# Newton's steps of the norm in PSUM, and adaLN slabs ahead of a SwiGLU's earliest quad

## The chip, the cores and the metric

The kernel runs on one core of a Trainium2 chip. The metric is device time in microseconds (us), the median of the runs shown. A core has five engines that work beside each other, each with its own queue of instructions executed in order: PE (products), DVE, ACT and POOL (elementwise work) and SP, which here only issues DMAs. They wait for each other through semaphores. Products write to PSUM, which DVE and ACT can read and write; all else lies in SBUF.

## What is computed

One step of a diffusion backbone of two layers on 640 tokens (512 latent, 128 context) of width 1024. Each layer is a SwiGLU, a mixer and a second SwiGLU, each behind a modulated norm:

```python
def rms_norm(x, g):
    y = x * lax.rsqrt(jnp.mean(x * x, axis=-1, keepdims=True) + EPS)
    return y * g
def modulate(h, shift, scale):
    return h * (1 + scale) + shift
def swiglu(h, w_gate, w_up, w_down):            # width 1024 -> 2816 -> 1024
    return (jax.nn.silu(h @ w_gate) * (h @ w_up)) @ w_down
mod = silu(cond) @ w_ada[l] + b_ada[l]          # nine vectors of 1024 a layer: shift, scale, gate x 3
x = x + 0.5 * mod[2] * swiglu(modulate(rms_norm(x, g[0]), mod[0], mod[1]), ...)
x = x + mod[5] * mixer(modulate(rms_norm(x, g[1]), mod[3], mod[4]))
x = x + 0.5 * mod[8] * swiglu(modulate(rms_norm(x, g[2]), mod[6], mod[7]), ...)
```

The mixers (neighbourhood attention with a recurrence; a Fourier transform) lie outside the change.

## The kernel before

**Tiling.** Channels lie on partitions, eight chunks of 128; the tokens are two halves of 320 columns (h = 0 and 1). A float32 product is three passes: weights and activations are split into a high and a low part, and high x high, low x high and high x low are summed. ACT makes a weight's high part (whi, line 176), DVE the low part (wlo, line 181), from a staging buffer (st) that a DMA on SP's queue fills (line 139). Buffers, and with them the loads, come free when the work that reads them is done; SP issues loads strictly in the planned order.

**Norm.** Sums of squares come from small products into a PSUM bank (nst, line 402). DVE turns three columns of them into 1/sqrt: v (line 415), a first guess on the bits (line 417), then three Newton steps of three operations each (lines 420, 421, 422), all on 128 x 3 values. Three operations spread the factors on a diagonal (dg, line 430), and products with ones bring them to all partitions (nbc, line 453). From nbc each chunk of h is made: x times nbc (line 473, or 469 in one step), the modulation (lines 476 and 479), the high part hh (lines 471 and 481) and the low part hl (lines 492 and 495).

**SwiGLU.** The inner width is 22 chunks. Chunks 0 and 1 are done directly in `ffn_body`: four units of weights (gate and up of each) times half 0 and then times half 1, in steps n as the norm gives chunks of h. Chunks 2 to 21 are "quads": gate and up of one chunk form a 2 x 2 matrix for Strassen's and Winograd's seven products. A quad's weights need sums (POOL, lines 226, 227, 231, 232) and six steps that split them (A1's whi and wlo come first). `prep(upto, 1)` takes one such step. The token side needs sums too (line 528, POOL and DVE) and their splits (th line 171, tl line 172). `norm_steps` is a generator that yields after each chunk; it is called for half 1 while the products of half 0 run: at step n = 1 DVE's Newton for half 1 is queued, at n = 4 nbc and the first three chunks, and the rest one chunk at each step of half 1, where PE takes each as it comes. Half 0's own SiLU (line 728) and product (729) come between the third and the fourth chunk of half 1.

**Slabs.** The nine vectors a layer are products with w_ada, cut in 144 slabs of 512 KB, eight to a vector (`fill`, line 327). They have no place of their own but fill PE's gaps. Three of the four SwiGLUs place some: 0ffn2 (layer 0, second; half 1's norm near 846 us of the trace), 1ffn1 (near 1315) and 1ffn2 (near 1861). `FILLS` gives for these the slabs at the first four steps of half 1 (two each; one each in 1ffn2) and after each quad. `plan_ffn` writes the order of the loads: in before the earliest quad's gate and up, then these eight (four) slabs, then the rest.

Of the kernel before, what the change touches and what calls it, by code (L numbers as in the profile page):

```python
# [32 lines left out]
class Item:  # L33
    """weights of one product: their loads, the steps that split them, what the steps made"""
# [7 lines left out]
class Kern:  # L42
# [21 lines left out]
    def buffers(self, pool, phase, n_st, n_w):  # L64
        """buffers for weights: as loaded, and split; those of a phase serve its weights only"""
        for j in range(n_st):
            self.st_free.append((pool.tile([P, 1024], F32, name=f"st{j}"), phase))
        for j in range(n_w):
            self.w_free.append((pool.tile([P, 1024], F32R, name=f"whi{j}"),
                                pool.tile([P, 1024], F32R, name=f"wlo{j}"), phase))  # L70
# [14 lines left out]
    def slab_pool(self, st, upto, bufs=2):  # L85
        """weights of the adaLN vectors: slabs up to this one are used in the phase"""
        self.slab_p = st.enter_context(self.tc.tile_pool(name="slab", bufs=bufs))
        self.s_dma = self.s_use
        self.s_end, self.s_bufs = upto, bufs

    def psum(self, pairs):
        """PSUM of a phase: six single banks or three pairs"""
        if self.ps_pairs is pairs:
            return
        self.ps_st.close()
        self.ps_pairs = pairs
        ps = self.ps_st.enter_context(self.tc.tile_pool(name="ps", bufs=3 if pairs else 6, space=PSUM))
        if pairs:
            self.pair = lambda name: ps.tile([P, 2, 512], F32, tag="mm", name=name)
            self.bank = lambda name: self.pair(name)[:, 0, :]  # L100
        else:
            self.bank = lambda name: ps.tile([P, 512], F32, tag="mm", name=name)
# [48 lines left out]
    def prep(self, upto, most=99):  # L151
        """steps for the items up to this one, as far as there are buffers"""
        self.flush()
        self.load()
        while self.steps and most:
            it, fn, need = self.steps[0]
            if it.idx >= min(upto, self.limit) or len(it.raw) < len(it.src) and fn in (self.split_w, self.quad_a, self.fold_a):
                return
            w = None
            if need:  # L160
                w = self.pick(self.w_free if need == 1 else self.s1_free, it.slots)
                if w is None:
                    return
            self.steps.pop(0)
            self.flush()
            fn(it, w)
            most -= 1
            self.load()
# [5 lines left out]
    def split_later(self, it, hi, lo, src, then=None):  # L174
        """the low part comes with the next step"""
# [20 lines left out]
    def fold_a(self, it, w):  # L196
        """rows m and -m: sum and difference"""
# [12 lines left out]
    # a pair of units as a 2 x 2 matrix (unit, half of the rows): the seven left factors of Strassen and Winograd  # L210
# [59 lines left out]
    def done(self, most=99):  # L270
        """the oldest unit in use is no longer needed"""
# [3 lines left out]
    def mm3(self, out, w, ks, xs, first=True, last=True):  # L275
        """out (+)= W^T X in three passes; w: (hi, lo) as [P, k, 128], xs: k -> (hi, lo)"""
# [8 lines left out]
    def mm_side(self, outs, ws, h, lag=0):  # L285
        """products of several units with half h, chunk after chunk as the norm gives them; the last two unit by unit
        lag: chunks by which the last unit stays behind"""
# [57 lines left out]
    def ada_end(self):  # L345
        """the finished vector, channels on partitions"""
# [28 lines left out]
    def parts(self, h):  # L375
        """pieces of a token half with one condition: (column slice, condition)"""
# [20 lines left out]
    def norm_s(self, h, bank=None):  # L397
        """sums of squares, tokens on partitions"""
# [6 lines left out]
    def norm_a(self, h):  # L405
        """rsqrt(mean(x^2) + eps)"""
# [4 lines left out]
    def rsqrt(self, ps, n=3):  # L411
        """rsqrt(mean(x^2) + eps) of n columns of sums"""
        nc = self.nc
        v, s, t_ = (self.t2.tile([P, 3], F32, tag=t, name=t)[:, :n] for t in ("nv", "ns", "nt"))
        nc.vector.tensor_scalar(out=v, in0=ps[:, 0:n], scalar1=1.0 / D, scalar2=EPS, op0=ALU.mult, op1=ALU.add)
        # the exponent halved on the bits, then Newton's steps
        nc.vector.tensor_scalar(out=s.bitcast(I32), in0=v.bitcast(I32), scalar1=-0.5, scalar2=float(0x5F3759DF),
                                op0=ALU.mult, op1=ALU.add)
        for _ in range(3):
            nc.vector.tensor_tensor(out=t_, in0=s, in1=s, op=ALU.mult)  # L420
            nc.vector.scalar_tensor_tensor(out=t_, in0=t_, scalar=-0.5, in1=v, op0=ALU.mult, op1=ALU.mult)
# [16 lines left out]
    def T_pool(self, ks=range(4)):  # L438
        """right factors of Strassen and Winograd beside the parts of h"""
# [9 lines left out]
    def norm_r(self):  # L449
        """the factors of the tokens on all partitions"""  # L450
# [6 lines left out]
    def norm_high(self, h, l, i, c, r, keep):  # L457
        """h = rms_norm(x) g (1 + scale) + shift and its high part
        keep: for the products of a SwiGLU"""
# [24 lines left out]
    def direct(self, l, i, h, c, keep):  # L484
        """the high part comes without the sum of product and shift"""
# [19 lines left out]
    def norm_steps(self, h, l, i, keep=False):  # L505
        """a step for each chunk, low parts one step behind"""
# [17 lines left out]
    def t_sums(self, k, b12, b22):  # L524
        """T1 = B12 - B11, T2 = B22 - T1, T3 = B22 - B12, T4 = B21 - T2"""
# [21 lines left out]
    # slabs of a SwiGLU: after chunks of the first units, and after each quad  # L547
# [5 lines left out]
    def plan_ffn(self, l, n, s):  # L553
        """weights of a SwiGLU in the order of their use; s: the first slab, returns the next"""
# [22 lines left out]
        for bi, nb in enumerate(BLK):  # L577
            end = min(sum(BLK[:bi + 1]) + 1, NF)
            while f < end:
                self.add_quad(gt[f], up[f], ph, f == 2)  # L580
                if f == 2:
                    slabs(sum(first))
                slabs(rest[f - 2])
# [7 lines left out]
    def ffn(self, l, i, after, mid=iter(()), late=None):  # L591
        """after(h, c): what follows the last update of chunk c, half h; mid: steps of other work, one in each quad;
        late: what follows the last quad"""
# [14 lines left out]
    def ffn_start(self, evac):  # L608
        """the first products of all: the first two vectors of adaLN come chunk by chunk, the norm and the products follow"""
# [7 lines left out]
        def ada(c):  # L617
            """the vectors' values for a chunk, four sums in groups of columns"""
# [102 lines left out]
    def ffn_body(self, l, i, fills, qfills, after, mid, late):  # L721
# [14 lines left out]
        if fills:  # L736
            us = [self.unit() for _ in range(4)]
            for h in range(2):
                ps = [self.bank("pg") for _ in us]
                for n, j in self.mm_side([p[:, :HT] for p in ps], us, h, 0 if h else LAG):  # L740
                    if j == 3:
                        self.prep(self.n_use + 1, 1)
                    if j == 3 and h == 0:
                        if n == 1:
# [5 lines left out]
                    elif j == 3:  # L750
                        step(1)
                        if n < 4:
# [44 lines left out]
    def down_last(self, fs, gate, after):  # L797
        """the last product before a norm: half 0 is through while four chunks of half 1 remain
        the first sums wait for the last chunk of the inner width"""
# [20 lines left out]
    def quad(self, f, fills, begin=False):  # L820
        """gate and up of a chunk, both halves of the tokens, in seven products
        M1 = A11 B11, M2 = A12 B21, M3 = S4 B22, M4 = A22 T4, M5 = S1 T1, M6 = S2 T2, M7 = S3 T3;
        C11 = M1 + M2, U2 = M1 + M6, C12 = U2 + M5 + M3, C21 = U2 + M7 + M4, C22 = U2 + M7 + M5"""
# [73 lines left out]
    def out_last(self, xs, gate, after):  # L897
        """the last product before a norm: half 0 is through while four chunks of half 1 remain"""
# [32 lines left out]
    def mix_setup(self):  # L931
        """parameters of the mixer, log_sigmoid(lambda)"""
# [13 lines left out]
        # y = |lam|, w = exp(-y) by halving steps and a series  # L946
# [17 lines left out]
        # log1p(w) = 2 artanh(w / (2 + w))  # L964
# [11 lines left out]
        # -2 log_sigmoid = 2 (2 artanh) - 2 min(lam, 0)  # L976
# [24 lines left out]
    def lru(self, c, xc, gel):  # L1001
# [21 lines left out]
        for d in range(2):  # L1023
            # exp(-z) and t = tanh(z / 2): 1 - a = t (1 + a), 1 - a^2 = t (1 + a)^2
# [28 lines left out]
    def qk_norm(self, which, c, ps):  # L1053
        """RMS norm over each head's 64 channels; q also gets -1/8"""
# [47 lines left out]
    def mixer0(self, after):  # L1102
        nc, tc = self.nc, self.tc
        self.bg, self.fg = [], []
        with ExitStack() as st:
# [18 lines left out]
            with ExitStack() as s2:  # L1124
# [60 lines left out]
                def early():  # L1185
                    """work that the first tiles of the attention cover"""
# [41 lines left out]
    def bias(self, c, v):  # L1228
        """mask less position bias of a variant of the windows' columns"""
# [122 lines left out]
    def fourier_const(self):  # L1352
        """the DFT matrices in the place of the right factors, a step for each piece"""
# [18 lines left out]
        def steps():  # L1372
# [9 lines left out]
            # the shift times the root of the number of tokens, by chunk in the group, group, condition  # L1382
# [10 lines left out]
    def scaled(self, h, c):  # L1393
        """x g (1 + scale) in parts; the factors of the tokens follow the channels' transform"""
# [12 lines left out]
    def fourier_front(self, const):  # L1407
        """what follows the updates before the transform"""
# [25 lines left out]
    def tok_rest(self):  # L1434
        """factors of the other tokens; the third tile has the end of half 0 and the start of half 1"""
# [8 lines left out]
    def fourier(self, after):  # L1444
        nc, tc = self.nc, self.tc
        NP, NQ, MP, MQ = self.NP, self.NQ, self.MP, self.MQ
        with ExitStack() as st:
# [6 lines left out]
            with ExitStack() as s2:  # L1454
# [11 lines left out]
                def chan(k, g):  # L1466
                    """the channels' transform: token tile k, group g"""
# [9 lines left out]
                def chan_out(k, g):  # L1477
                    """times the factors of the tokens, in parts"""
# [26 lines left out]
                # the shift's part, the same for all tokens  # L1505
# [25 lines left out]
                def pos(r):  # L1531
                    """rows r: cosines of group r, 4 the Nyquist channels, 5 + g sines of group g"""
# [9 lines left out]
                    def shift(q):  # L1542
                        """the shift stays at the first position"""
# [18 lines left out]
            with ExitStack() as s2:  # L1562
# [14 lines left out]
                for c in range(KD):  # L1577
# [17 lines left out]
                    # token n has the sum, the one as far from the end the difference  # L1595
# [16 lines left out]
    def run(self, stop=99):  # L1612
        nc, a = self.nc, self.a
        const = self.const
        with self.tc.manual_schedule():
# [54 lines left out]
            def after(l, i, first=4, per=3, keep=True):  # L1670
                """the next norm: half 0 while the last products of half 1 run"""
# [49 lines left out]
def pack(inp):  # L1721
    """lays the inputs out; no arithmetic"""
# [9 lines left out]
    # the first two vectors by chunks of channels  # L1732
# [47 lines left out]
    # DFT matrices: channels (columns: cosines 0..127, the first halved, cosine 128, sines 1..127) and positions  # L1780
# [37 lines left out]
```

## Time and profile before

| what | us |
|---|---|
| median of 3 runs (2305.37 to 2310.3) | 2305.5 |
| span of the profiled execution | 2305.0 |
| PE, PE weight load, DVE busy | 2224.0, 2110.0, 1554.8 |
| ACT, POOL busy | 990.7, 954.9 |
| PE waiting for dg ahead of nbc, 7 times, the longest | 7.8, 3.4 |
| PE waiting for wlo with pg's products, 3 times, the longest | 5.0, 2.6 |

Busy rows count how long an engine had an instruction in work. A row of the timeline is start, duration, engine, line, operation, output<-input, and in brackets how long the engine had been idle and what ended it. A row of the waits is who waited <- for whom: us in total, times, the longest. A group's row gives count and minimum/median/maximum duration in ns. A row of DMA issues ends with the median us from issue to landing; a row of a stage's window gives the busy times of PE, PE's weight loads, DVE, ACT and POOL, the clock granted to PE (1.00 is full), the share of the DMA engines and GB/s.

### The profile page before, as it was taken

How to read it: one execution, taken by the hardware profiler on the slowest of the kernel's cores; microseconds unless marked ns; L12 is line 12 of the kernel's file. 1: busy time of each engine (PE TensorE's matmuls, PEld its weight loads, DVE VectorE, ACT ScalarE, POOL GpSimd, SP SyncE). 2: the span in 40 equal slices, each digit the busy share in tenths (PEclk: the TensorE clock that was granted, in tenths of full speed). 3: DMA queues.
4: the chain of work that ended last, by engine and by line, in shares of the span. 5: the costliest groups of instructions: out<-in, count | busy, mean ns of one | idle time of the engine just before them, and what ended most of it. 6: DMA issues, size and time to landing. Idle time of an engine off the chain costs nothing.

```text
span 2305.0 us, 39901 instructions
## 1 busy us (share of the span) xinstructions
PE 2224.0 (96%) x15534; PEld 2110.0 (92%) x15534; DVE 1554.8 (67%) x2871; ACT 990.7 (43%) x1780; POOL 954.9 (41%) x856
## 2 busy tenths in 40 slices
PE   7999999999998899999999999999999989999999
PEld 5889999999994788999999889999999979999999
DVE  6676677666865368666666786666667786666665
ACT  4433333347855435333333453333335553333332
POOL 2444444440023235444444454444443645444441
PEclk9999999999999999999999999999999999999999
DMA  7333333321228424333322243332332322222221
GB/s 278 113 111 105 105 107 107 115 74 56 73 71 267 131 83 137 110 101 110 106 91 97 75 155 120 110 97 96 103 117 62 128 85 83 83 83 83 83 89 57
DMA packets 75316, 245.44 MB, mean 106 GB/s; under 512 B 8756, under 2 KB 12996, under 8 KB 75128
## 3 DMA queue, kind: packets, MB, share of 16 engines
q1 hardware_dynamic: 74168, 241.28, 31.7%
q8 instruction: 123, 2.02, 0.4%
q10 hardware_dynamic: 864, 1.38, 0.2%
q14 instruction: 65, 0.53, 0.1%
q0 software_dynamic: 96, 0.22, 0.0%
HBM read 239.71 MB, written 3.15 MB: 105 GB/s over the span
## 4 chain that ended last, share of the span: by engine, by line
PE 79%; DVE 13%; ACT 4%; issue 2%; POOL 2%; DMA 1%; ACTq 0%; DVEq 0%; SPq 0%; POOLq 0%
PE q L282 40%; PE pd L282 26%; PE pj L282 5%; DVE wlo L181 2%; PE ada L327 2%; DVE tl L172 1%; PE pg L282 1%; PE gt L1014 1%; PE pos L1549 1%; DVE x L381 1%; PE S L1262 1%; DVE y L473 1%; DVE sx L1268 1%; PE PT L1288 1%; DMA st<-w_ada 1%
## 5 line engine op out<-in xcount | busy, mean ns | idle before, releaser
L181 DVE TENSOR_TENSOR wlo<-st,whi 128x1024 fp32r<-128x1024 f32 (+2 forms) x401 | 498.4, 1254 | 11.1 <-ACT whi L176 10.2
L176 ACT ACTIVATE whi<-st 128x1024 fp32r<-128x1024 f32 (+2 forms) x405 | 401.2, 992 | 233.0 <-POOL st L232 139.3
L282 PE MATMUL pd<-g,whi 128*128 128x320 f32 x1536 | 347.0, 310 | 4.3 <-DVE u L825 2.3
L381 DVE SCALAR_TENSOR_TENSOR x<-pd,mods,x 128x128 f32<-128x128 f32 (+2 forms) x696 | 265.0, 433 | 111.7 <-PE pd L282 111.2
L282 PE MATMUL q<-hh,wlo 128*128 128x320 f32 x960 | 296.9, 309 | 5.3 <-DVE wlo L181 5.3
L282 PE MATMUL q<-hh,whi 128*128 128x320 f32 x960 | 300.7, 313 | 1.0 <-DVE u L825 1.0
L282 PE MATMUL q<-th,whi 128*128 128x320 f32 x960 | 297.3, 310 | 3.0 <-DVE sg L825 3.0
L282 PE MATMUL q<-tl,whi 128*128 128x320 f32 x960 | 296.6, 309 | 0.7 <-POOL tl L172 0.7
L282 PE MATMUL q<-th,wlo 128*128 128x320 f32 x960 | 296.6, 309 | 0.0
L282 PE MATMUL q<-hl,whi 128*128 128x320 f32 x960 | 296.3, 309 | 0.0
L231 POOL TENSOR_TENSOR st<-sums,st 128x512 f32<-128x512 f32 x80 | 118.0, 1474 | 396.9 <-DVE wlo L181 359.5
L825 POOL TENSOR_TENSOR u<-u,u 128x320 f32<-128x320 f32 x80 | 106.5, 1331 | 401.0 <-DVE u L825 401.0
L282 PEld LDWEIGHTS pd<-g,whi 128*128 128x128 f32 x1536 | 256.8, 188 | 8.9 <-DVE x L381 3.1
L282 PE MATMUL pd<-hh,whi 128*128 128x320 f32 x768 | 238.4, 310 | 0.0
L282 PE MATMUL pd<-hl,whi 128*128 128x320 f32 x768 | 237.9, 310 | 0.0
L282 PE MATMUL pd<-g,wlo 128*128 128x320 f32 x768 | 237.7, 310 | 0.0
L282 PE MATMUL pd<-hh,wlo 128*128 128x320 f32 x768 | 236.8, 308 | 0.0
L826 ACT ACTIVATE sg<-sg 128x320 f32<-128x320 f32 x160 | 75.4, 471 | 284.5 <-DVE sg L825 284.5
L282 PEld LDWEIGHTS q<-hh,whi 128*128 128x128 f32 x960 | 180.2, 188 | 16.8 <-issue 8.6
L282 PEld LDWEIGHTS q<-th,whi 128*128 128x128 f32 x960 | 180.3, 188 | 6.6 <-issue 4.7
L282 PEld LDWEIGHTS q<-hh,wlo 128*128 128x128 f32 x960 | 180.2, 188 | 6.4 <-DVE wlo L181 6.4
L282 PEld LDWEIGHTS q<-tl,whi 128*128 128x128 f32 x960 | 180.4, 188 | 1.5 <-POOL tl L172 1.5
(327 smaller groups left out, 5016.0 us busy)
## 6 DMA issues: line engine op xcount, KB each, us to landing
st<-w_ada SPq DMA_DIRECT2D x144, 512.0 KB, 4.6
st<-ffn_gate SPq DMA_DIRECT2D x88, 512.0 KB, 3.6
st<-ffn_up SPq DMA_DIRECT2D x88, 512.0 KB, 3.7
st<-ffn_down SPq DMA_DIRECT2D x96, 384.0 KB, 3.1
st<-w_in SPq DMA_DIRECT2D x20, 512.0 KB, 3.5
st<-ffn_down SPq DMA_DIRECT2D x16, 512.0 KB, 3.5
st<-w_out_ab SPq DMA_DIRECT2D x8, 512.0 KB, 3.5
st<-w_out_c SPq DMA_DIRECT2D x8, 512.0 KB, 3.5
```

What stands on the lines that cost most here:

```text
L172: (eng or self.nc.vector).tensor_tensor(out=lo, in0=src, in1=hi.bitcast(F32), op=ALU.subtract)
L176: self.nc.scalar.activation(out=hi, in_=src, func=AF.Copy)
L181: self.low.tensor_tensor(out=lo, in0=src, in1=hi.bitcast(F32), op=ALU.subtract)
L231: self.nc.gpsimd.tensor_tensor(out=s[:, 0:512], in0=it.s1, in1=s[:, 0:512], op=ALU.subtract)
L282: self.nc.tensor.matmul(out, lhsT=l, rhs=r, start=first and j == 0, stop=last and j == len(ops) - 1)
L327: nc.tensor.matmul(self.ada_ps[32 * j:32 * j + 32, 0:256], lhsT=self.s_sb[:, k, :], rhs=t[:, 256 * j:256 * j + 256], start=k == 0, stop=k ...
L381: self.nc.vector.scalar_tensor_tensor(out=self.x[h][c][:, sl], in0=ps[:, sl], scalar=gate[:, c, r:r + 1], in1=self.x[h][c][:, sl], op0=ALU ...
L473: nc.vector.tensor_tensor(out=y, in0=self.x[h][c], in1=r, op=ALU.mult)
L825: tt = lambda e, o, a, b, op=ALU.add: e.tensor_tensor(out=o, in0=a, in1=b, op=op)
L826: cp = lambda o, p, fn=AF.Copy: nc.scalar.activation(out=o, in_=p, func=fn)
L1014: nc.tensor.matmul(g[:, s, 0:322], lhsT=wt[:, d, j, :], rhs=xc[:, 322 * s:322 * s + 322], start=True, stop=True)
L1262: nc.tensor.matmul(o, lhsT=q, rhs=k, start=True, stop=True)
```

## The change

Three things; the rest of the text's difference are removed comments, which move line numbers above 743 by 5.

```diff
 def rsqrt(self, ps, n=3):
-        v, s, t_ = (self.t2.tile([P, 3], F32, tag=t, name=t)[:, :n] for t in ("nv", "ns", "nt"))
+        v, s, t_ = (x[:, :n] for x in (ps[:, 4:8], self.t2.tile([P, 3], F32, tag="ns", name="ns"), ps[:, 8:12]))
...
         for _ in range(3):
-            nc.vector.tensor_tensor(out=t_, in0=s, in1=s, op=ALU.mult)
-            nc.vector.scalar_tensor_tensor(out=t_, in0=t_, scalar=-0.5, in1=v, op0=ALU.mult, op1=ALU.mult)
+            nc.vector.tensor_tensor(out=t_, in0=v, in1=s, op=ALU.mult)
+            nc.vector.scalar_tensor_tensor(out=t_, in0=t_, scalar=-0.5, in1=s, op0=ALU.mult, op1=ALU.mult)
             nc.vector.scalar_tensor_tensor(out=s, in0=t_, scalar=1.5, in1=s, op0=ALU.add, op1=ALU.mult)
...
 def plan_ffn(self, l, n, s):
-                self.add_quad(gt[f], up[f], ph, f == 2)
                 if f == 2:
                     slabs(sum(first))
+                self.add_quad(gt[f], up[f], ph, f == 2)
                 slabs(rest[f - 2])
...
 def ffn_body(self, l, i, fills, qfills, after, mid, late):
-                    if j == 3:
+                    if j == 3 and h == 0 and n < 4:
+                        self.flush()
+                        self.load()
+                    elif j == 3:
                         self.prep(self.n_use + 1, 1)
                     if j == 3 and h == 0:
+                        if n in (2, 3):
+                            self.fill(fills.pop(0))
                         if n == 1:
...
                     elif j == 3:
                         step(1)
-                        if n < 4:
+                        if n < 2:
                             self.fill(fills.pop(0))
```

In all twelve norms v and t_ move into columns 4 to 12 of the PSUM bank of the sums, so that each operation has at most one input in SBUF. In the three SwiGLUs with fills, the earliest quad's steps start at n = 4 of half 0 instead of n = 0, half of the slabs move from half 1 to steps 2 and 3 of half 0, and the slabs' loads precede the loads of this quad's gate and up.

SP's loads in 0ffn2, in before (st is a staging buffer with its number, w_ada a slab):

```order
L139 DMA st_66<-ffn_gate 128x1024
L139 DMA st_65<-ffn_up 128x1024
L139 DMA st_64<-w_ada 128x1024
L139 DMA st_8449<-w_ada 128x1024
L139 DMA st_8450<-w_ada 128x1024
L139 DMA st_8451<-w_ada 128x1024
```

and now:

```order
L139 DMA st_66<-w_ada 128x1024
L139 DMA st_65<-w_ada 128x1024
L139 DMA st_64<-w_ada 128x1024
L139 DMA st_8439<-w_ada 128x1024
L139 DMA st_8440<-w_ada 128x1024
L139 DMA st_8441<-w_ada 128x1024
L139 DMA st_66<-w_ada 128x1024
L139 DMA st_65<-w_ada 128x1024
L139 DMA st_64<-ffn_gate 128x1024
L139 DMA st_8439<-ffn_up 128x1024
```

Slabs 0 and 1 take the two early places of gate and up, and gate now loads into st_64, the buffer of slab 2, after all eight slabs.

ACT in 0ffn2 now, from the end of half 0's norm (the rows are the same in before, but for the buffer, which was st_66; whi_69 is A1's high part, b_8562 and y are chunks of half 1):

```order
L471 ACTIVATE hh_101<-y,mods 128x320
L176 ACTIVATE whi_69<-st_64 128x1024
L479 ACTIVATE b_8562<-b_8562,mods,sc 128x192
L481 ACTIVATE hh_87<-b_8562 128x320
L479 ACTIVATE y<-y,mods,sc 128x192
L481 ACTIVATE hh_95<-y 128x320
L479 ACTIVATE b_8573<-b_8573,mods,sc 128x192
L481 ACTIVATE hh_89<-b_8573 128x320
L728 ACT_TABLE_LOAD
L728 ACTIVATE sg<-pg 128x320
```

Nothing moved here; the operation that stands ahead of half 1's chunks is the one that reads the gate.

PE in 0ffn2 around the first of the four slabs and around nbc, now (pg are the units' sums; between the pieces stand products of pg alone):

```order
L282 MATMUL pg<-hh_87,wlo_68 128x320
L327 MATMUL ada<-st_66,s_sb 32x256 x4
L327 MATMUL ada<-st_65,s_sb 32x256 x4
L282 MATMUL pg<-hh_93,whi_71 128x320
...
L282 MATMUL pg<-hh_89,wlo_68 128x320
L327 MATMUL ada<-st_64,s_sb 32x256 x4
L327 MATMUL ada<-st_8439,s_sb 32x256 x4
L282 MATMUL pg<-hh_95,whi_71 128x320
...
L282 MATMUL pg<-hh_91,wlo_68 128x320
L453 MATMUL nbc<-dg,ones 128x128 x2
```

In before none of these four L327 rows stood ahead of nbc. On DVE one wlo (wlo_70, A1's) moved from directly ahead of line 415 to behind half 1's first line 528, and on POOL the four sums moved from ahead of half 1's first two operations of line 528 to behind them.

## The prediction

> **What bounds the kernel now.** I read the page first, then PE's waits in the three stretches that the change touches, then each engine's rows there.
>
> ```profile
> span 2305.0 us, 39901 instructions
> PE 79%; DVE 13%; ACT 4%; issue 2%; POOL 2%; DMA 1%; ACTq 0%; DVEq 0%; SPq 0%; POOLq 0%
> ```
>
> PE carries 79% of the chain that ended last, so the change can win only where PE waits or runs slow, and lose wherever it makes PE wait. The change touches the second norm of the three SwiGLUs that carry fill slabs. PE's waits there, in 845 to 870 (0ffn2), 1312 to 1325 (1ffn1; the middle two rows) and 1853 to 1870 (1ffn2):
>
> ```profile
> PE nbc L453 <- DVE dg L430: 3.4, 1, 3.4
> ...
> PE pg L282 <- DVE wlo L181: 2.6, 1, 2.6
> PE nbc L453 <- DVE dg L430: 1.5, 1, 1.5
> ...
> PE nbc L453 <- DVE dg L430: 0.3, 1, 0.3
> ```
>
> The norm's factors come late because DVE's Newton steps stall. DVE in 0ffn2, and beside it POOL's sums of the earliest quad:
>
> ```profile
> 846.15 0.15 DVE L415 TENSOR_SCALAR nv<-nst 128x3 f32<-128x3 f32 x1
> 846.34 1.07 DVE L417 TENSOR_SCALAR ns<-nv 128x3 int32<-128x3 int32 x1
> ...
> 847.64 1.14 DVE L421 SCALAR_TENSOR_TENSOR nt<-nt,nv 128x3 f32<-128x3 f32 x1
> ...
> 852.09 0.77 DVE L430 TENSOR_SCALAR dg<-ident,ns 128x128 f32<-128x128 f32 x3
> ...
> 845.28 2.11 POOL L226 TENSOR_TENSOR sums<-st 128x512 f32<-128x512 f32 x1 [1.66 <-DMA st<-ffn_up]
> ```
>
> An undisturbed step takes 0.15 to 0.16 us and the next starts 0.19 after its start; several took about 1.1 while POOL worked, so the chain from L415 to dg took 5.94 us (846.15 to 852.09) where eleven free steps take 11 x 0.19 = 2.1. PE's price is the wait and a slow stretch behind it:
>
> ```profile
> 852.52 1.81 PE L453 MATMUL nbc<-dg,ones 128*128 128x128 f32 x6 [3.44 <-DVE dg L430]
> ...
> 855.22 0.47 PE L282 MATMUL pg<-hh,whi 128*128 128x320 f32 x1
> 855.49 0.47 PE L282 MATMUL pg<-hl,whi 128*128 128x320 f32 x1
> ...
> 859.53 0.31 PE L282 MATMUL pg<-hh,wlo 128*128 128x320 f32 x1
> 859.68 0.31 PE L282 MATMUL pg<-hh,whi 128*128 128x320 f32 x1
> ...
> 852.00:860.00 8.00, 7.48 (x30) 7.17 (x31) 4.53 (x13) 3.47 (x7) 1.75 (x2) 0.57 0.04 15
> ```
>
> After the wait products start every 0.27 us (the mean granted clock to 860 is 0.57), from 859.5 on every 0.15. From 855.2 to 859.5 that is 4.3 / 0.27 = 16 products, which lose 16 x 0.12 = 1.9 us. In 1ffn1 (below) nbc took 1.07 us instead of 1.81 after a wait of 1.53, so a short wait does not slow PE.
>
> **Newton's steps in PSUM.** Each step now has at most one input in SBUF. What such an operation does while POOL works is shown by L415 and by L473 (one input of nbc, in PSUM), against an operation with two SBUF inputs:
>
> ```profile
> L415 DVE TENSOR_SCALAR nv<-nst x12: 139/160/163, 12.1 to 1861.5; 128x3 f32<-128x3 f32 x11, 128x2 f32<-128x2 f32 x1
> L473 DVE TENSOR_TENSOR y<-x,nbc x36: 472/480/489, 501.3 to 1889.4; 128x320 f32<-128x320 f32 x36
> L421 DVE SCALAR_TENSOR_TENSOR nt<-nt,nv x36: 161/161/1145, 12.7 to 1865.1; 128x3 f32<-128x3 f32 x33, 128x2 f32<-128x2 f32 x3
> ...
> 13.90 0.71 DVE L421 SCALAR_TENSOR_TENSOR nt<-nt,nv 128x3 f32<-128x3 f32 x1
> 825.97 0.81 DVE L417 TENSOR_SCALAR ns<-nv 128x3 int32<-128x3 int32 x1
> ```
>
> PSUM operands never stall in 48 rows, and L415, from PSUM, is no dearer than L420 from SBUF. So I take stalls gone, other price nothing. That returns, outside the three stages, about 0.6 + 0.55 + 0.55 = 1.7 us at most in the start's chain (I take 1.0: PE is fed by loads there as well) and 0.65 before 829 (I take 0.3). [...] The sum goes by the rows: bounds -2.3 (all of both) to +0.3 (no return, and twelve steps of a norm dearer by L415's own spread, 163 less 139 ns); value -1.3.
>
> **The four slabs ahead of nbc, and the loads.** A pair of slabs is short work on PE:
>
> ```profile
> 864.62 1.07 PE L327 MATMUL ada<-st,s_sb 128*32 128x256 f32 x16
> ```
>
> Two pairs ahead of nbc, and two fewer after it, leave PE's sum as it was. In 0ffn2 Newton ends early: its second wlo is out of the way (-1.1) and the stalls are gone, so dg is done near 848.1. But nbc now stands behind slabs 2 and 3, which load where slabs 0 and 1 did:
>
> ```profile
> 845.17 1.75 SPq L139 DMA_DIRECT2D st<-w_ada  x4
> ...
> st<-w_ada SPq DMA_DIRECT2D x1, 512.0 KB, 3.5
> ...
> st<-w_ada SPq DMA_DIRECT2D x1, 512.0 KB, 4.4
> ...
> st<-w_ada SPq DMA_DIRECT2D x2, 512.0 KB, 7.2
> ```
>
> The four issues lie 0.44 us apart (1.75 / 4). The first of the four landed at 845.17 + 3.5 = 848.7, the second at 845.6 + 4.4 = 850.0, the last at 846.5 + 7.2 = 853.7. So slab 3 multiplies at 850.0 to 850.5, the 12 products of step n = 4 follow (12 x 0.15 = 1.8), and nbc starts near 852.3, where it was 852.52. The 3.4 us wait is filled, not moved: what comes back is the clock, 1.9 us, if anything uses it.
>
> What stands last next is the load of the quad's gate. Its buffer is that of slab 2, free near 849.2, and its transfer lies behind six slabs. Four landed by 853.7 in before; two more and the gate at 1.3 us each (850.0 less 848.7) make 857.6. If the four keep 1.3 us all the way the gate lands at 848.7 + 6 x 1.3 = 856.5; at the 1.85 us each of the last two (853.7 less 850.0, halved) at 859.2. ACT executes in order, and its next operation after half 0's norm is whi of this gate, then the second half's first L479:
>
> ```profile
> 843.02 1.04 ACT L176 ACTIVATE whi<-st 128x1024 fp32r<-128x1024 f32 x1
> 854.89 0.55 ACT L479 ACTIVATE b<-b,mods,sc 128x192 f32<-128x192 f32 x1 [10.82 <-DVE b L473]
> ...
> 857.51 0.47 ACT L481 ACTIVATE hh<-b 128x320 fp32r<-128x320 f32 x1
> 859.48 1.28 ACT L728 ACT_TABLE_LOAD   x1 [1.50 <-PE pg L282]
> ```
>
> So whi ends at 857.6 to 860.3, and L479 starts 2.7 to 5.4 us late. Queued behind whi are all six norm operations of the first three chunks and the SiLUs of half 0. The 1.5 us in which ACT waited for PE are absorbed (PE is early now), and the fourth chunk comes 1.2 to 3.9 late. The quad's four sums, the first of which took 2.11 us above, move beside it. The last row here is a stage's: PE, PEld, DVE, ACT, POOL busy, clock, DMA share:
>
> ```profile
> 866.21 0.90 POOL L528 TENSOR_TENSOR t<-hh,y 128x320 f32<-128x320 f32 x1 [7.05 <-DVE y L528]
> 868.28 1.16 DVE L495 TENSOR_TENSOR hl<-y,hh 128x320 fp32r<-128x320 f32 x1
> ...
> 882.83 0.42 PE L282 MATMUL pg<-hl,whi 128*128 128x320 f32 x1 [0.24 <-DVE hl L495]
> ...
> 870.00:884.00 14.00, 13.76 (x109) 11.76 (x108) 13.47 (x22) 7.12 (x17) 9.17 (x11) 1.00 0.61 219
> ```
>
> POOL had a 7 us hole there, yet DVE's two-SBUF operations beside POOL's take 1.16 instead of 0.48 (L495), so two or three of them and the moved wlo cost 0 to 2 us. From 870 on DVE is busy 13.47 of 14.00 us, and PE at the end waits for it only 0.24 us: a shift of that chain is a shift of the kernel, and slabs taken out of that half give nothing. 0ffn2: +1.2 to +5.9, value +3.
>
> 1ffn1 has no clock loss and no table load to absorb:
>
> ```profile
> 1313.98 1.75 SPq L139 DMA_DIRECT2D st<-w_ada  x4
> ...
> st<-w_ada SPq DMA_DIRECT2D x2, 512.0 KB, 6.7
> ...
> 1319.42 1.07 PE L453 MATMUL nbc<-dg,ones 128*128 128x128 f32 x6 [1.53 <-DVE dg L430]
> ...
> 1321.05 0.55 ACT L479 ACTIVATE b<-b,mods,sc 128x192 f32<-128x192 f32 x1 [9.78 <-DVE b L473]
> ...
> 1324.06 0.42 ACT L728 ACTIVATE sg<-pg 128x320 f32<-128x320 f32 x1
> ```
>
> POOL's sums no longer disturb the wlo that PE waited 2.6 us for, so I let the burst start 1.8 earlier, at 1312.2. Slab 3 lands at 1317, nbc comes near 1319.4, as before. The burst's last lands at 1312.2 + 1.3 + 6.7 = 1320.2, the gate three transfers later, 1324.1 to 1325.8 (all at 1.3: 1323.5), and L479 starts 3.5 to 5.8 late. Value +4.5 with the wlo and collisions, bounds +2.5 to +7.
>
> 1ffn2 has four slabs, whose gate load goes to a free buffer and blocks nobody; nbc there waited 0.3 us and now has two slabs (1.07) ahead: +0.5 to +3, value +1.
>
> Sum: -1.3 + 3 + 4.5 + 1 = +7.2. The profiled execution spans 2305.0, and the median of the runs is 2305.5, the same within 0.02%, so I forecast 2312.7. Ends: -2.3 + 1.2 + 2.5 + 0.5 = +1.9, and +0.3 + 5.9 + 7 + 3 = +16.2.
>
> **The rivals.** *Gate in time, nothing gained* (same): the loads run without backlog, ACT isn't held, and nbc waits for slabs instead of for dg. It speaks for this that the first transfer of a burst takes 3.5 us, against it that the later ones took 4.4 and 7.2. The price is -1.3 + 1 and collisions of 0 to 2: about 2306.
>
> *Gate in time, the clock used* (faster): if the gate lands by 853.8 in 0ffn2 and 1320 in 1ffn1, whi is over before L479 is ready. The evacuations then come up to 1.9 us earlier in 0ffn2 (ACT's 1.5 us wait for pg is what could shrink, and DVE's after it), the 1.8 us of the wlo in 1ffn1 come through to half 1, and the start gives 1.3: 2305.5 - 5.0 = 2300.5. For it speaks that PE's waits are real and go; against it the queue of six slabs.
>
> *PSUM steps dear* (slower still): if steps on PSUM are dearer by as much as the stalls took, the 1.3 us do not come back, and the sum is 7.2 + 1.3 = +8.5, or 2314. L415's and L473's rows speak against it. [...]
>
> **How the numbers follow.** A measurement of this kernel can tell about 0.2%, 4.6 us, from no change. My forecast has 0.58 (0.50 above +4.6, 0.08 within), the second 0.20 (0.15 within, 0.03 faster, 0.02 slower), the third 0.17 (0.14 faster, 0.03 within), the last 0.05, slower. Faster 0.17, same 0.26, slower 0.57. The range 2300.5 to 2320 leaves out about half of the third case and the top of the first, since bounds of the parts will hardly all meet.
>
> **What would show it.** Right: the Newton steps at 0.16 us throughout; nbc of 0ffn2 near 852 behind two slabs with no wait over 1.5 us and a clock of 1.00 after it; ACT idle before A1's whi until the gate's landing, that whi ending after 857, and the first L479 of half 1 directly after it in 0ffn2 and 1ffn1. Wrong: whi over before DVE's first L473 of half 1; L479 at or before 854.9 and 1321.0; steps above 0.2 us; or the fourth chunk's L473 no later than its 864.5 while PE reaches the end of half 1 earlier.

## The result: slower by 1.28%, four times what was forecast

The changed kernel takes 2335.32 us (median of 4 runs, 2334.21 to 2339.79), where the kernel before took 2306.47 beside it: a ratio of 1.0128, 95% interval 1.0116 to 1.014, some 29 us. The forecast was +7.2, its range ended at 2320.

The span, and PE's longest waits over the whole of the changed kernel (who waits <- for whom: us in total, times, the longest):

```profile
span 2338.0 us, 39902 instructions
PE adaT L353 <- ACT adaev L340: 29.6, 4, 10.5
PE PT L1293 <- DVE sx L1284: 14.6, 20, 3.6
...
PE pg L282 <- DVE wlo L181: 2.5, 3, 1.3
...
PE nbc L453 <- DVE dg L430: 1.9, 3, 0.8
```

nbc's wait for dg fell from 7.8 to 1.9 us and that of pg for wlo from 5.0 to 2.5: what the change was seen to remove is removed. But a wait of 29.6 us now leads the list, and the prediction doesn't have it. In it PE, about to transpose a finished adaLN vector (adaT), waits for ACT's copy of that vector out of PSUM (adaev). It happens once in each of the three stages (9.1, 10.5 and 9.8 us); in the profile of before it came to 0.3 in all:

```profile
PE adaT L353 <- ACT adaev L340: 0.3, 1, 0.3
```

Newton's operations in the changed kernel (count, minimum/median/maximum ns):

```profile
L420 DVE TENSOR_TENSOR nst<-nst,ns x36: 169/170/170, 12.8 to 1887.0; 128x3 f32<-128x3 f32 x33, 128x2 f32<-128x2 f32 x3
L421 DVE SCALAR_TENSOR_TENSOR nst<-nst,ns x36: 168/170/170, 13.0 to 1887.2; 128x3 f32<-128x3 f32 x33, 128x2 f32<-128x2 f32 x3
L422 DVE SCALAR_TENSOR_TENSOR ns<-nst,ns x36: 160/161/163, 13.2 to 1887.4; 128x3 f32<-128x3 f32 x33, 128x2 f32<-128x2 f32 x3
```

No step stalls any more; the two that write to PSUM take 9 ns longer than in SBUF (170 against 161).

0ffn2 on ACT. At 815 us, ahead of the stage, PE runs 4.0 us later than in the profile of before by what had happened earlier; "on the clock of before" below means that this shift (each kernel's own) is taken off:

```profile
845.99 0.55 ACT L471 ACTIVATE hh<-y,mods 128x320 fp32r<-128x320 f32 x1
860.71 1.06 ACT L176 ACTIVATE whi<-st 128x1024 fp32r<-128x1024 f32 x1 [14.18 <-DMA st<-ffn_gate]
861.68 0.53 ACT L479 ACTIVATE b<-b,mods,sc 128x192 f32<-128x192 f32 x1
...
882.49 0.47 ACT L481 ACTIVATE hh<-b 128x320 fp32r<-128x320 f32 x1
882.87 0.46 ACT L171 ACTIVATE th<-y 128x320 fp32r<-128x320 f32 x1
883.23 0.45 ACT L171 ACTIVATE th<-t 128x320 fp32r<-128x320 f32 x1
883.59 0.36 ACT L340 ACTIVATE adaev<-ada 128x256 f32<-128x256 f32 x1
```

and on PE, with the loads on SP's queue as the last two rows:

```profile
852.08 0.64 PE L327 MATMUL ada<-st,s_sb 128*32 128x256 f32 x8 [0.17 <-DMA st<-w_ada]
853.38 0.64 PE L327 MATMUL ada<-st,s_sb 128*32 128x256 f32 x8 [0.66 <-DMA st<-w_ada]
...
855.82 0.97 PE L453 MATMUL nbc<-dg,ones 128*128 128x128 f32 x6
...
871.91 1.07 PE L327 MATMUL ada<-st,s_sb 128*32 128x256 f32 x16
872.91 0.42 PE L282 MATMUL pg<-hh,whi 128*128 128x320 f32 x1
884.00 0.69 PE L353 MATMUL adaT<-ident,adaev 128*128 128x128 f32 x2 [9.06 <-ACT adaev L340]
884.34 0.61 PE L282 MATMUL pg<-hh,whi 128*128 128x320 f32 x1
884.75 0.47 PE L282 MATMUL pg<-hl,whi 128*128 128x320 f32 x1
885.02 0.47 PE L282 MATMUL pg<-hh,wlo 128*128 128x320 f32 x1
...
838.75 12.64 SPq L139 DMA_DIRECT2D st<-w_ada  x8
852.78 0.33 SPq L139 DMA_DIRECT2D st<-ffn_gate  x1
```

The forecast's steps are all there: slabs 2 and 3 multiply as they land, nbc follows at 855.82 (851.8 on the clock of before), the gate is issued when slab 2 is through, whi waits 14.18 us for it, and half 1's first L479 comes directly behind, at 857.7 on the clock of before instead of 854.89. Then comes what is new: the last two slabs are multiplied at 871.9, one group of twelve products follows, and PE stands before the transposition until 884.00, because adaev stands on ACT behind seven of the norm's eight chunks. Behind the wait products start every 0.27 us, where the twelve ahead of it start every 0.15; the granted clock from 884.34 to 889.82 is 0.50.

How much each stage lost is read by the n-th product of PE in both traces: the shift of its start between a point ahead of the stage and one behind it (815 to 935 us of before, 1280 to 1400, 1840 to 1950). For all kernels of this study, us against before:

| kernel | 0ffn2 | 1ffn1 | 1ffn2 | three stages | median, us |
|---|---|---|---|---|---|
| changed kernel | +8.4 | +11.5 | +8.5 | +28.4 | 2335.3 |
| e1_newton_psum | -6.0 | -1.8 | -0.7 | -8.5 | 2302.0 |
| e2_transpose_late | +2.8 | +6.9 | +2.9 | +12.6 | 2322.1 |
| e3_evac_one_chunk_earlier | +6.9 | +9.9 | +6.5 | +23.3 | 2331.9 |
| e4_slabs_late | +3.6 | +6.2 | +3.6 | +13.4 | 2322.4 |
| e5_split_behind_norm | +3.0 | +6.4 | +6.3 | +15.7 | 2324.5 |
| e6_only_delay | -5.1 | -1.4 | +1.4 | -5.1 | 2305.0 |
| e7_gate_after_six | +0.3 | +5.3 | +3.4 | +9.0 | 2316.8 |
| e8_psum_delay_two | -5.7 | -0.8 | -0.1 | -6.6 | 2302.7 |
| e9_psum_delay_three | -5.9 | -0.2 | -0.2 | -6.3 | 2302.2 |
| e10_psum_transpose_early | +3.5 | +8.3 | +8.4 | +20.2 | 2331.8 |
| e11_newton_sbuf | +3.2 | +6.2 | +3.3 | +12.7 | 2320.1 |

The rest of a profile moves by -1.4 to +5.2 us between executions, most of it between 400 and 815, in the attention, where PE waits up to 3.6 us at a time: the profiled execution of the changed kernel lost 5.2 us there against that of before, in code of which the change touches only the norms. Medians of before were 2306.5 to 2307.4 beside these kernels.

### The profile page after: what moved, and what is told of

Read it like the earlier page. It is cut to its first block, busy times and chain, and to the rows that moved or that the text cites. A ratio compares the mean times of both kernels' runs of the same rounds, so it can differ in the third digit from the quotient of the medians.

```text
span 2338.0 us, 39902 instructions
## 1 busy us (share of the span) xinstructions
PE 2234.0 (96%) x15534; PEld 2118.7 (91%) x15534; DVE 1548.9 (66%) x2871; ACT 992.1 (42%) x1780; POOL 960.0 (41%) x856
## 4 chain that ended last, share of the span: by engine, by line
PE 80%; DVE 11%; ACT 4%; issue 2%; DMA 2%; POOL 2%; SPq 0%; ACTq 0%; DVEq 0%; POOLq 0%
PE q L282 40%; PE pd L282 26%; PE pj L282 5%; DVE wlo L181 2%; PE ada L327 2%; PE pg L282 2%; PE S L1267 1%; PE gt L1019 1%; DVE tl L172 1%; PE pos L1554 1%; DMA st<-w_ada 1%; DVE x L381 1%; DVE sx L1273 1%; DVE sx L1284 1%; PE PT L1293 1%
## 5 line engine op out<-in xcount | busy, mean ns | idle before, releaser
L282 PEld LDWEIGHTS pd<-g,whi 128*128 128x128 f32 x1536 | 257.6, 188 | 10.2 <-DVE x L381 4.0
L282 PEld LDWEIGHTS q<-hh,whi 128*128 128x128 f32 x960 | 180.2, 188 | 15.8 <-issue 9.1
L282 PEld LDWEIGHTS q<-th,wlo 128*128 128x128 f32 x960 | 180.4, 188 | 2.3 <-DVE wlo L181 2.3
```

Of the source, the lines that this page charges most:

```text
L282: self.nc.tensor.matmul(out, lhsT=l, rhs=r, start=first and j == 0, stop=last and j == len(ops) - 1)
```

## The experiments

Theory A: the loss is the sum of two things, the transposition that PE now meets early while its input stands late on ACT, and the gate's late load that holds ACT (the forecast's own mechanism). Theory B: the gate's load holds the whole second half, and the wait for adaev only stands where waits for hh and hl would stand otherwise. Two more come with the runs that test them. Theory C: slabs in the first steps of half 1 cost something by themselves. Theory D: the quad's delayed steps collide with half 1's chunks on DVE and POOL. In kernels with the edit to `shift` (e2, e5, e7, e11) every line behind it has a number higher by 1 (L480 there is L479).

**Newton's values in PSUM, alone** (e1). The three lines of `rsqrt` of the change, in the kernel before.

> The kernel before with Newton's two values in PSUM and nothing else changed. All theories: no Newton step over 0.2 us, though POOL's sums still run beside them in 0ffn2, 1ffn1 and 1ffn2; the chain from L415 to the last L422 takes 2.1 to 2.4 us in all twelve norms. Newton being 3.8 us shorter in 0ffn2, nbc's wait of 3.4 us there falls under 0.5, PE keeps its clock, and with the start's 1.3 us the time is 2298 to 2303, faster than before by 3 to 8 us. [...]

2301.95 us (10 runs), a ratio of 0.9978 (0.9969 to 0.9987). Its steps beside POOL's sums:

```profile
L421 DVE SCALAR_TENSOR_TENSOR nst<-nst,ns x36: 168/170/170, 13.1 to 1858.5; 128x3 f32<-128x3 f32 x33, 128x2 f32<-128x2 f32 x3
...
PE nbc L453 <- DVE dg L430: 0.6, 1, 0.6
```

In 0ffn2 nbc waits 0.6 us instead of 3.4 (second row; under 0.5 was expected), and that stage alone gives 6.0 us. So this third of the change is a gain, and the other two lose some 33 us.

**The transposition put back** (e2).

```diff
     def shift(self, l, i):
-        self.ada_end()
+        if self.ada_m and self.ada_m[0] in (9 * l + 3 * i, 9 * l + 3 * i + 1):
+            self.ada_end()
```

> The changed kernel, but asking for a shift vector no longer flushes a finished vector that is another one, so the transposition adaT goes back to where it stood in the kernel before, behind all products of half 1. Theory A (the transposition stands on PE ahead of the last five steps of half 1 while its input stands on ACT behind seven of eight chunks of the norm): the three waits of 9 to 10.5 us go with the half clock behind them, and the time falls by 25 to 30 us to 2305 to 2311. Theory B (the gate's late load holds ACT and with it the whole chain of half 1, and the transposition's wait only stands in for it): PE then waits for hh and hl of half 1 instead, and the time stays above 2325.

2322.06 us, a ratio of 1.0064 (1.005 to 1.0077): 13 us of the 29 are gone, and neither theory has its number. PE's waits over the whole of this kernel:

```profile
PE PT L1294 <- DVE sx L1285: 13.4, 19, 3.6
PE pg L282 <- DVE hl L496: 12.2, 10, 2.8
```

No wait of adaT for adaev in the three stages is left; in its place stand waits for hl (2.9 in before, 12.2 here). Most of these, 8.3, also come with the held steps alone (e6 below). The edit also shows why the transposition moved. `norm_high` asks for the shift at each chunk, and `shift` flushed whatever vector was finished, needed or not. The fourth and fifth chunk of half 1 are queued right behind half 0, so the last three come at steps 0, 1 and 2 of half 1. In before the eighth slab came at step 3, after the last chunk had asked, at step 2; so the flush waited until the earliest quad, either for its own flush behind the last of its seven products or, in 1ffn1, for the next vector's first slab. In 0ffn2 of before PE met it here, with no wait:

```profile
897.10 0.38 PE L353 MATMUL adaT<-ident,adaev 128*128 128x128 f32 x2
```

Now the eighth slab comes at step 1, the last chunk asks at step 2, and adaT stands there in PE's queue, 144 products earlier (120 in 1ffn1).

**The same by the slabs' place** (e4): in half 1 `if n in (2, 3)` instead of `if n < 2`.

> The changed kernel with the four slabs of half 1 at its steps 2 and 3 instead of 0 and 1, so that the vector is finished after the last shift was asked for and the transposition stands late without any other edit. Theory A (transposition 13 us, gate and whi the rest): the same as the run with the transposition put late, 2319 to 2325, no wait for adaev over 1 us. Theory C (slabs in the first steps of half 1 matter themselves): clearly off it, under 2317 or over 2327.

2322.35 us, as e2. Two edits that share only the transposition's place give the same time; theory C falls.

**The copy one chunk earlier** (e3).

```diff
-                        step(1)
                         if n < 2:
                             self.fill(fills.pop(0))
+                        step(1)
```

> The changed kernel, with the fill of half 1 ahead of the norm's step instead of behind it, so that ACT copies the finished vector one chunk of the norm earlier, and the transposition stands one group of twelve products earlier on PE. Theory A: PE's wait for adaev ends one chunk (3.5 to 4 us) earlier in each of the three stages, but starts up to 1.8 us earlier too; what counts is its end, so the time falls by 8 to 12 us to 2323 to 2327. Theory B: nothing in the gate's load or whi changes, so 2333 to 2337.

2331.89 us, -3.4 (-5.1 in the three stages) where theory A had -8 to -12 and B nothing. adaev did come 3.3 us earlier in 0ffn2 (876.3 on the clock of before, 879.6 in the changed kernel), but the transposition stands twelve products earlier, so 1.8 us more work lies behind it: 3.3 less 1.8 is 1.5 a stage, as measured (1.5, 1.6, 2.0). The direction is A's; the size was mine to work out and I left the group out.

**The transposition alone, early** (e10): e1 with `if n == 3: self.ada_end()` behind the fill of half 1; slabs and loads as before.

> The kernel before with Newton's values in PSUM, and nothing else of the change, but the finished vector is transposed right behind the eighth slab in half 1, where ACT's copy of it (adaev) stands behind the norm's last chunk. If the transposition alone makes the 13 us that were missing in the forecast: PE waits 8 to 9 us for adaev in each of the three stages, four groups of twelve products follow late (4 x 1.8, part of them at half clock), so 4 to 6 us a stage, 2314 to 2320 where the kernel without it took 2302. If PE would have waited for the norm's chunks anyway, under 2306.

2331.81 us, 30 more than e1 and nearly the changed kernel's time, out of the transposition alone. PE and ACT in 0ffn2:

```profile
866.10 1.07 PE L327 MATMUL ada<-st,s_sb 128*32 128x256 f32 x16
876.08 0.69 PE L353 MATMUL adaT<-ident,adaev 128*128 128x128 f32 x2 [8.91 <-ACT adaev L340]
...
872.47 0.47 ACT L481 ACTIVATE hh<-y 128x320 fp32r<-128x320 f32 x1
875.66 0.37 ACT L340 ACTIVATE adaev<-ada 128x256 f32<-128x256 f32 x1
```

The stages lose 9.5, 10.1 and 9.1 us against e1, about the whole wait (8.9, 8.5 and 10.2; behind it, in 0ffn2, products start every 0.27 us instead of 0.15): where PE is just in time with the norm's chain, hardly anything of it overlaps. I had expected half, having counted four groups of products behind it; PE's next wait ends at 890.55, so some 13 us of work stands behind the transposition.

**The gate two slabs earlier** (e7): e2 with `slabs(min(6, sum(first)))` ahead of the earliest quad and the rest behind.

> The run with the transposition late, and the quad's gate and up loaded after six of the eight slabs instead of after all (in 1ffn2, with four slabs, nothing changes). The gate then waits for slab 0's buffer instead of slab 2's and has two transfers fewer ahead. Theory A: it lands 3 to 4.5 us earlier in 0ffn2 and 1ffn1, whi and L479 come as much earlier, and the time falls by 5 to 8 us to 2314 to 2317. Theory D: nothing, 2320 to 2324.

2316.79 us, 5.3 less than e2, as theory A had it and not D. In 0ffn2:

```profile
855.42 1.06 ACT L176 ACTIVATE whi<-st 128x1024 fp32r<-128x1024 f32 x1 [11.58 <-DMA st<-ffn_gate]
856.38 0.53 ACT L480 ACTIVATE b<-b,mods,sc 128x192 f32<-128x192 f32 x1
```

On the clock of before half 1's first chunk starts at 855.1 on ACT, 0.2 after that of before, and the stage loses 0.3; in e2 it starts 2.9 late (857.8) and loses 2.8; in e1 4.2 early (850.7), and gains 6.0. In these kernels the stage follows the start of this operation (not in e5, next). It came 2.7 us earlier than in e2 here and 1.7 in 1ffn1, less than the 3 to 4.5 that were expected, and these stages are 2.5 and 1.6 better.

**whi behind the norm's chunks** (e5): e2 with the quad's steps from n = 6 on (`n < 6` for `n < 4`).

> The run with the transposition late, and the earliest quad's steps start two steps later, at n = 6 of half 0: ACT reaches A1's whi after the three first chunks of half 1 and the first SiLU, by when the gate is in; loads and slabs stay. Theory A (what remains of the loss, 15 us, is whi waiting on ACT for the gate): ACT's 14 us idle ahead of whi goes, L479 of half 1 starts when DVE's L473 is ready, the fourth chunk is 3 to 5 us earlier in 0ffn2 and 1ffn1, and the time is 2306 to 2313. Theory D (the quad's delayed steps collide with half 1's chunks on DVE and POOL, which is what makes the rest): still later steps, so no gain, 2320 to 2326.

2324.45 us: theory D's number. ACT was freed as A said: half 1's first chunk started at 853.5 on the clock of before, 4.3 earlier than in e2. But POOL's sums now ran among the later chunks, and DVE's operations with two inputs in SBUF beside them:

```profile
870.86 1.26 POOL L226 TENSOR_TENSOR sums<-st 128x512 f32<-128x512 f32 x1
872.20 1.40 POOL L227 TENSOR_TENSOR st<-st,st 128x512 f32<-128x512 f32 x1
...
870.90 1.57 DVE L496 TENSOR_TENSOR hl<-b,hh 128x320 fp32r<-128x320 f32 x1
872.39 1.56 DVE L529 TENSOR_TENSOR y<-y,b 128x320 f32<-128x320 f32 x1
...
881.07 0.49 DVE L529 TENSOR_TENSOR b<-b,hh 128x320 f32<-128x320 f32 x1 [2.01 <-POOL t L529]
```

Where such an operation takes 0.48 free, it takes 1.57 here. So the run moved two costs against each other and decides nothing by its time: the rows show A's mechanism and D's, each at its place, but not what each is worth.

**Only the delay** (e6): Newton in PSUM and the quad's steps from n = 4; slabs and loads as before.

> The kernel before with Newton's values in PSUM and the earliest quad's steps held until the second norm's factors, but slabs and loads as before: the gate is loaded before it is wanted, and the transposition stands late. Theories A and B both: no wait for adaev and none of whi for the gate, 2298 to 2306. It tells what holding the sums is worth: against the run with Newton's values alone, a gain of 1 to 2 us if the wlo and POOL's sums still cost something ahead of nbc, a loss of 1 to 3 if they collide with half 1's chunks.

2305.01 us, 3 more than e1. Holding the sums buys nothing and costs these 3 us: PE waits 8.3 us for hl instead of 2.4. Against e6, e2 adds the early slabs and their loads: 17 us, 7.9 and 8.3 of it in 0ffn2 and 1ffn1. How much of that is the gate's late load and how much the slabs themselves is known only for the two loads that e7 moved.

**Shorter delays** (e8, e9): e1 with the quad's steps held for two and for three steps.

> The kernel before with Newton's values in PSUM, and the earliest quad's steps held for two steps of half 0 instead of four; loads and slabs as before. The last wlo of the four units should be clear of POOL's sums in 1ffn1 (PE waited 2.6 us for it), while the sums run beside the Newton steps, which they can't disturb any more, and end before half 1's chunks. 2298 to 2302 if so; if the sums now collide with half 1's chunks as in the run with the whole delay, 2303 to 2306.

> The kernel before with Newton's values in PSUM, and the earliest quad's steps held for three steps of half 0; loads and slabs as before. Half of POOL's sums now stand ahead of half 1's first line 528 and half behind. If holding the sums is worth anything ahead of nbc (the wlo that waits 2.6 us in 1ffn1), 2299 to 2301; if it only brings them among half 1's chunks, between the run with Newton's values alone (2302) and that with the whole delay (2305).

2302.66 and 2302.19 us: no different from e1. PE's wait for wlo in 1ffn1 stays at 2.6 with two steps.

**Newton back in SBUF** (e11): e2 with `rsqrt` as before.

> The run with the transposition late (2322), with Newton's values back in SBUF. With the sums held until half 1, nothing of POOL runs beside Newton in the three stages, and nbc waits for slabs anyway, so only the start and the norm near 826 lose: 2322 to 2325. If Newton's gain in PSUM, 8 us in the three stages of the kernel before, were also in the changed kernel, 2328 to 2332.

2320.13 us, a ratio of 1.0057 (1.0044 to 1.0071), not told apart from e2's 1.0064; the stages lose 12.7 us with Newton in SBUF and 12.6 with it in PSUM. So the 8.5 us of e1 aren't in the changed kernel. Newton's steps in 0ffn2 of this run:

```profile
845.96 0.15 DVE L416 TENSOR_SCALAR nv<-nst 128x3 f32<-128x3 f32 x1
846.14 0.17 DVE L418 TENSOR_SCALAR ns<-nv 128x3 int32<-128x3 int32 x1
846.54 0.16 DVE L422 SCALAR_TENSOR_TENSOR nt<-nt,nv 128x3 f32<-128x3 f32 x1
848.11 0.77 DVE L431 TENSOR_SCALAR dg<-ident,ns 128x128 f32<-128x128 f32 x3
```

In SBUF too, no step of the three stages takes over 0.17 us, and from L416 to dg these rows take 2.15 us, against 5.94 in before: POOL's sums run later, and none of its operations lies beside these steps. Holding the sums removes the stalls by itself, and besides, nbc stands behind slabs.

## Why the prediction was right in its direction and wrong in its size

- *Newton.* Right that the stalls go and that a PSUM operand is hardly dearer (9 ns on two steps of three). Of the -1.3 outside the stages, the norm near 826 gave more than its 0.3: PE's shift falls by 0.6 us from 815 to 840 in every kernel with the edit, and not in e11 (the table counts this with 0ffn2). The start's 1.0 wasn't shown: the part to 400 us moved by -1.4 to +0.1 between kernels that share the edit. And two stretches without any Newton step, 935 to 1280 and 1950 to the end, are 0.3 and 0.7 us longer in every kernel with the edit, and not in e11; the cause is open. Newton's worth in the stages was real, 8.5 us without the other edits (e1), and nothing with them (e11). The prediction saw that nbc behind slabs would hide it; that the held sums alone end the stalls there it did not say.
- *nbc filled, not moved.* Right: near 852.3 forecast, 851.8 found.
- *The gate holds ACT.* Right. whi ended at 857.8 on the clock of before (857.6 to 860.3 forecast); L479 was 2.8 late in 0ffn2 (2.7 to 5.4) and 4.3 in 1ffn1 (3.5 to 5.8). Without the transposition the stages lose 2.8, 6.9 and 2.9 (e2; 3.6, 6.2 and 3.6 in e4), where the values were 3, 4.5 and 1; but for the last in e4 they lie within their bounds, and e7 shows the mechanism. In 1ffn2, where the gate holds nobody, the steps' delay alone makes 2.1 of it (e6 +1.4, e1 -0.7).
- *The step that failed* is "Two pairs ahead of nbc, and two fewer after it, leave PE's sum as it was", with "slabs taken out of that half give nothing". I moved the slabs and not what the eighth of them sets off: ACT's copy, and PE's transposition at the next flush. Both were in the order of the changed kernel, where adaT stands 144 products earlier on PE. That is 29.4 us of waiting in the three stages and, by e2 and e4, 13 us of the median (15.8 in the profiles' stages). The other half overlaps with a chain that is late anyway; e10, where the chain is not late and the transposition alone costs 30 us, speaks for this.
- *What is left without it.* e2 is still 14.7 us above the kernel before beside it (2307.36), twice the +7.2 and past the end of the range. Of the 7.5 us between, 4.4 are in the table's three stretches (12.6 against 3 + 4.5 + 1 and the -0.3 near 826; 1ffn1 has 2.4 of them, 1ffn2 1.9), 1.0 is the start's return that wasn't seen, and 2.1 are not traced. So the sum was too low even for what it covered.
- *The clock.* I expected 1.00 behind nbc since a wait of 1.5 us had done no harm. In the changed kernel a wait of 2.26 us (866.56, for the SiLU) was followed by half pace (0.27 us from product to product instead of 0.15), and so was each wait for adaev, also at 0.27 us: in 0ffn2 for the 21 products from 884.34 to 889.82, an estimated 2.5 us if nothing of it overlaps, in 1ffn1 to 1364.38 and in 1ffn2 to 1920.67. How much of the 13 us that is was not separated.
- *The rivals.* None held. The faster one failed on its condition, since whi could start only at 856.7 on the clock of before, not by 853.8; "PSUM steps dear" is refuted by the rows (170 ns at most, where the longest stalled steps took 1145).

## What to carry to other kernels

When work is moved, list all that its last piece sets off on other engines, and find where each of these now stands in each queue: a short operation whose input stands late in another engine's queue can cost the whole distance (30 us in e10; 13 where other work was late too). A flush called for safety from an unrelated place moves with the data's readiness, so its place in the queue is nobody's decision. And edits that serve the same wait don't add up: Newton in PSUM and the held sums each end the stalls, and the slabs were to fill the wait that these had already emptied.

Newton's values in PSUM alone is the version that beats both kernels, 2301.95 us.

## What the runs showed that was not expected

In the changed kernel PE's products started every 0.27 us instead of 0.15 behind a wait of 2.26 us; in the kernel before, behind a wait of 2.6 us, they went on every 0.15:

```profile
866.56 0.64 PE L282 MATMUL pg<-hh,whi 128*128 128x320 f32 x1 [2.26 <-ACT sg L728]
864.00:870.00 6.00, 3.74 (x26) 2.25 (x24) 4.52 (x9) 3.68 (x7) 4.88 (x5) 0.72 0.00 1
...
1313.96 0.42 PE L282 MATMUL pg<-hh,wlo 128*128 128x320 f32 x1 [2.62 <-DVE wlo L181]
1312.00:1321.00 9.00, 5.52 (x35) 5.07 (x36) 7.91 (x17) 0.00 (x0) 3.41 (x3) 1.00 0.64 232
```

The first two rows are the changed kernel's 2.26 us wait and the stretch around it (granted clock 0.72), the last two those of before with the 2.6 us wait (1.00). In e4 the same 2.26 us wait was followed by three products at full pace, and only from 864.05 on by half pace:

```profile
863.50 0.42 PE L282 MATMUL pg<-hh,whi 128*128 128x320 f32 x1 [2.26 <-ACT sg L728]
863.76 0.31 PE L282 MATMUL pg<-hl,whi 128*128 128x320 f32 x1
864.05 0.58 PE L282 MATMUL pg<-hh,whi 128*128 128x320 f32 x1
864.42 0.47 PE L282 MATMUL pg<-hl,whi 128*128 128x320 f32 x1
```

So in these runs the length of the wait alone does not decide whether the pace halves; what else does was not shown.

Between 680 and 700 us and between 760 and 790, in the attention, the granted clock was 0.91 and 0.83 in the profiled execution of the changed kernel, and 1.00 and 0.94 in that of before.
